# POOL's early arithmetic moved to DVE, and the rotary tables queued behind the rows' factors, in a hybrid decoder layer

## The chip, the core and the metric

The kernel runs on one core of a Trainium2 chip. Its engines work beside one another, each through its own queue in order: PE (matrix products; PEld is its loading of weights), DVE and ACT (work on whole tiles), POOL (the same, and DMAs of its own), SP (issues DMAs). The metric is the device time of one execution in microseconds; the profile is of one more execution, recorded instruction by instruction.

## What is computed

One decoder layer in float32 on 512 tokens of width 1024. The stretch that matters here is its beginning:

```python
u = rms_norm(h, norm_mix_g[l])
proj = u @ w_in[l]
conv_in, c_q, c_kv, k_rope_raw, gate_logits = jnp.split(proj, cut, axis=-1)
# conformer_conv, over conv_in: 512 channels, 31 taps
a, gt = jnp.split(conv_in, 2, axis=-1)
z = a * jax.nn.sigmoid(gt)
z = lax.conv_general_dilated(z, rhs, ..., feature_group_count=CONV_CH)
# rope_tables, used by the MLA attention
ang = positions.astype(jnp.float32)[..., None] * inv_freq
return jnp.cos(ang), jnp.sin(ang)
```

After it come the layer norm of the conv branch, the MLA attention, the gated merge, a cross-attention over 256 memory tokens and an MLP, with a final norm.

## The kernel before

**Products.** Every float32 product is made of three: each operand is split into a high half (rounded, on ACT, or scaled on ACT for x) and a low half (the rest, by a subtraction), and `mm3` (L231) sums high by high, low by high and high by low in one PSUM bank. `split` (L201) makes the two halves of weights: L202 is the copy on ACT, L203 the subtraction, on the engine `eng` or on DVE. `split_scaled` (L205) does the same for x times a norm's gain: L206 on ACT, L207 on DVE. PSUM has eight banks; products with the tag `mm` share four of them.

**First tile.** The loop at L610 goes over the eight 128-row slices k of x as they arrive: it splits the slice (`split_x`, L207 for the low half `ul`), splits the weights of the slices (`split` at L619, for k = 1, 2, 4, 6, with POOL for the low half), and PE multiplies at L622 into two banks, `fa` (the conv value) and `fg` (its gate). These are the first of the four channel tiles (index 0 to 3, `("ag", c)`).

**Rows' factors of x.** PE multiplies x without its RMS factor; the factor comes later. `x_stats` (L575) squares the slices on ACT (L577) and adds them up in turns on DVE and POOL (L579), and POOL adds the two sums into `nacc` (L580). `x_rows` (L582) sums `nacc` over the partitions on PE (L277), and DVE makes 1/sqrt from it in twelve small operations on 128x4 (L279, L245 to L250) into `rx`; a thirteenth makes `rx2` (L584). `x_bcast` (L586) spreads `rx` over the partitions with four transposes on PE (L271) and a copy on ACT to `rbx` (L588), evacuates the gate of tile 0 (`evac_g`, L599: L601 on DVE, the sigmoid L602 on ACT, L603 and L604 on DVE), and calls `rope_tables`.

**Rotary tables.** `rope_tables` (L439) makes the angles of the rotary embedding, reduced to one turn: 23 DVE operations on 128x4 to 128x64 (L440 to L462). `rope_sin` takes sine and cosine of them on ACT (L467, L468); nothing else reads them before the keys are turned, far later.

**Order.** PE's order is as written. `Pipe` (L337) prepares a unit's weights one unit ahead; `w_eng` is the engine of their subtraction: DVE for tile 1, POOL for tiles 2 and 3 and the units behind them. `after(ticks, fn)` (L214) puts work behind so many groups of three products: `x_bcast` stands five behind the row sums (D_X), hence in the middle of the gate of tile 1. The order on DVE, ACT and POOL is a planner's: it goes by readiness, by modelled durations and by the order in which the code writes the operations, and may put a later operation ahead of one that is not ready. The conv taps (`conv_taps`, L486: L492 once, L494 thirty times per tile, on DVE) run as background beside the products, and so do the gates' evacuations (L721) and the factors of the two latents (`latent_rows`, L669).

Of the kernel before, what the change touches and what calls it, by code (L numbers as in the profile page):

```python
# [19 lines left out]
ALU = mybir.AluOpType  # L20
# [148 lines left out]
def _body(tc, a):  # L169
# [3 lines left out]
    dve = nc.vector  # L173
    act = nc.scalar
    gps = nc.gpsimd
# [25 lines left out]
    def split(hi, lo, src, eng=None):  # L201
        act.copy(hi, src)  # L202
        (eng or dve).tensor_tensor(lo, src, hi.bitcast(F32), op=ALU.subtract)  # L203
# [14 lines left out]
    def tick(w):  # L218
        nonlocal bg
        clock[0] += w  # L220
        while later and later[0][0] <= clock[0] and not clock[2]:
            heapq.heappop(later)[2]()
        bg(w)
# [37 lines left out]
    rx = cst.tile([P, NT], F32, name="rx")  # L261
    rx2 = cst.tile([P, NT], F32, name="rx2")
# [5 lines left out]
    def bcast_rows(r, n=NT):  # L268
        b = bank("at")
        for t in range(n):  # L270
            pe.transpose(b[:, t * P:(t + 1) * P], r[:, t:t + 1].to_broadcast([P, P]), ident)  # L271
        return b

    def rstd_rows(sq, dim, dst=None):
        b = bank("at")
        for t in range(NT):
            pe.matmul(b[:, t:t + 1], sq[:, t * P:(t + 1) * P], ones1, start=True, stop=True)  # L277
        v = sm.tile([P, NT], F32, tag="rv", name="rv")
        dve.tensor_scalar(v, b[:, :NT], 1.0 / dim, EPS, op0=ALU.mult, op1=ALU.add)  # L279
        r = sm.tile([P, NT], F32, tag="rr", name="rr") if dst is None else dst  # L280
        rsqrt(r, v, NT)
        return r
# [11 lines left out]
    raws = {}  # L294
# [37 lines left out]
    w_eng = [dve]  # L332
# [32 lines left out]
    xr = xp.tile([P, KD, S], F32, name="xr")  # L365
    nacc = xp.tile([P, S], F32, name="nacc")
# [62 lines left out]
    def split_x(k):  # L429
        split_scaled(uh[:, k, :], ul[:, k, :], xr[:, k, :], v_("norm_mix_g", k))  # L430
# [8 lines left out]
    def rope_tables():  # L439
        dve.tensor_copy(posf, posi)  # L440
        fr = kon[:, K_FREQ:K_FREQ + n]
        for t in range(NT):
            sl = slice(16 * t, 16 * t + 16)
            dve.tensor_scalar(ang[:, sl], fr[:, sl], posf[:, t:t + 1], None, op0=ALU.mult)

        def fma(k, c):
            dve.scalar_tensor_tensor(ang, k, -c, ang, op0=ALU.mult, op1=ALU.add)

        dve.tensor_scalar(k_, ang, 1.0 / TWO_PI, MAGIC, op0=ALU.mult, op1=ALU.add)
        dve.tensor_scalar(k_, k_, MAGIC, None, op0=ALU.subtract)  # L450
        dve.tensor_scalar(kh, k_, 2.0 ** -11, MAGIC, op0=ALU.mult, op1=ALU.add)
        dve.tensor_scalar(kh, kh, MAGIC, 2048.0, op0=ALU.subtract, op1=ALU.mult)
        dve.tensor_tensor(k_, k_, kh, op=ALU.subtract)
        for c in PI_PARTS:
            fma(kh, c)
            fma(k_, c)
        dve.tensor_scalar(k_, ang, 1.0 / TWO_PI, MAGIC, op0=ALU.mult, op1=ALU.add)
        dve.tensor_scalar(k_, k_, MAGIC, None, op0=ALU.subtract)
        for c in PI_PARTS:
            fma(k_, c)  # L460
        dve.tensor_scalar(ang, ang, 3.1415925, -3.1415925, op0=ALU.min, op1=ALU.max)
        dve.scalar_tensor_tensor(k_, ang, -1.0, ang, op0=ALU.mult, op1=ALU.max)  # L462
# [103 lines left out]
    def proj_unit(key, c0, evac):  # L566
        def main(hl):
            b = bank()
            mm3(b, [(lhs(hl, k), (uh[:, k, :], ul[:, k, :])) for k in range(KD)])
            evac(b)  # L570
        pipe.unit(lambda: prep(key, c0=c0), main)

    hold = {}

    def x_stats():  # L575
        for k in range(KD):
            act.activation(xr[:, k, :], xr[:, k, :], AF.Square)  # L577
            if k > 1:
                (dve, gps)[k % 2].tensor_tensor(xr[:, k % 2, :], xr[:, k % 2, :], xr[:, k, :], op=ALU.add)  # L579
        gps.tensor_tensor(nacc, xr[:, 0, :], xr[:, 1, :], op=ALU.add)  # L580

    def x_rows():  # L582
        rstd_rows(nacc, D, rx)
        dve.tensor_tensor(rx2, rx, rx, op=ALU.mult)  # L584

    def x_bcast():  # L586
        b = bcast_rows(rx)
        act.copy(rbx, b)  # L588
        hold["a"] = fa
        evac_g(fg, 0)  # L590
        act.copy(identb, ident)
        act.copy(maskb, kon[:, K_MASK:K_MASK + 128])
        rope_tables()


    def evac_a(b, c):
        hold["a"] = b

    def evac_g(b, c):  # L599
        sg = wkp.tile([P, S], F32, tag="sg", name="sg")  # L600
        dve.tensor_tensor(sg, b, rbx, op=ALU.mult)  # L601
        act.activation(sg, sg, AF.Sigmoid)  # L602
        dve.tensor_tensor(sg, sg, rbx, op=ALU.mult)  # L603
        dve.tensor_tensor(zpad[:, c, CW - 1:], hold["a"], sg, op=ALU.mult)  # L604
        zready[0] = c + 1
# [4 lines left out]
    for k in range(KD):  # L610
        hl = first[k // 4]
        if k == 0:
            dve.tensor_copy(hl[0][:, 0], raws[0][:, 0])
            dve.tensor_tensor(hl[1][:, 0], raws[0][:, 0], hl[0][:, 0].bitcast(F32), op=ALU.subtract)
        split_x(k)
        if k == 1 or k > 0 and k % 2 == 0:
            kn = 1 if k == 1 else 2
            sl = slice(k % 4, k % 4 + kn)
            split(hl[0][:, sl], hl[1][:, sl], raws[0][:, k:k + kn], gps)  # L619
        for i, j in ((0, 0), (1, 0), (0, 1)):  # L620
            for b, c0 in ((fa, 0), (fg, 128)):
                pe.matmul(b, hl[i][:, k % 4, c0:c0 + 128], (uh, ul)[j][:, k, :],  # L622
                          start=k == 0 and i == j == 0, stop=k == KD - 1 and j == 1)
        tick(2.0)
    pipe.ahead(lambda: prep(("ag", 1), c0=0))
    x_stats()

    def evac_a1(b):
        x_rows()
        hold["a1"] = b  # L630
        after(D_X, x_bcast)
# [3 lines left out]
        evac_g(b, 1)  # L635

    for c in range(1, CT):
        w_eng[0] = dve if c == 1 else gps
        proj_unit(("ag", c), 0, evac_a1 if c == 1 else lambda b, c=c: evac_a(b, c))
        proj_unit(("ag", c), 128, evac_g1 if c == 1 else lambda b, c=c: evac_g(b, c))  # L640
    pipe.flush()
# [193 lines left out]
    for t in range(NT):  # L835
        b = bank()
        sl = slice(t * P, (t + 1) * P)
# [700 lines left out]
```

## Time and profile before

| | us |
|---|---|
| median of three runs | 796.04 (795.7 to 796.46) |
| the profiled execution | 797.19 |
| its span, first to last instruction | 795.4 |
| PE busy | 761.3 (96%) |
| DVE busy | 535.3 (67%) |
| ACT busy | 400.6 (50%) |
| POOL busy | 169.7 (21%) |

Busy time says how much of the span an engine worked, not whether anything waited for it. The chain of waits does: it is followed back from the last instruction to whatever released it. "Granted clock" is the share of TensorE's full 2.4 GHz that the chip gave PE in a stretch. The span begins with the loads of x and of the first weights, and the stretch that the change touches is its first 40 us.

### The profile page before, as it was taken

The page shows a single profiled execution, that of the slowest core. Times are in us where ns is not written, and L with a number is a line of the kernel's source. Part 1 is how long each engine was busy: PE and PEld are TensorE (multiplying, and loading weights), DVE is VectorE, ACT ScalarE, POOL GpSimd, SP SyncE. Part 2 cuts the span into 40 slices and gives each one's busy share as a digit, 9 for nine tenths or more (in the row PEclk, how much of TensorE's full clock was granted, in tenths as well). Part 3 has the DMA queues.
Part 4 walks back from the last instruction along what each step waited for, and adds up shares of the span by engine and source line. Part 5 has one row for each costly group of instructions (what it writes and reads, how often), then busy time and mean ns, then how long its engine had stood idle before and what let it go on. Part 6 is the DMA issues. An engine that isn't in the chain of part 4 may idle for free.

```text
span 795.4 us, 9520 instructions
## 1 busy us (share of the span) xinstructions
PE 761.3 (96%) x3594; PEld 627.8 (79%) x3594; DVE 535.3 (67%) x812; ACT 400.6 (50%) x681; POOL 169.7 (21%) x103
## 2 busy tenths in 40 slices
PE   8799999999999998998999999999999979999996
PEld 4589788778788886788887888888888858888785
DVE  5798999843888859758686833243333446667995
ACT  7323333469666537343465644444343445655562
POOL 4444336423312215346320000000000000111000
PEclk9899999999999999899999999999999998999998
DMA  8213223222102144124132324425353596999731
GB/s 280 97 40 113 76 84 128 84 90 97 54 0 107 54 157 162 58 102 146 68 105 106 118 108 146 171 82 224 106 188 129 165 283 239 227 236 213 198 106 53
DMA packets 26989, 103.36 MB, mean 130 GB/s; under 512 B 2368, under 2 KB 9920, under 8 KB 17984
## 3 DMA queue, kind: packets, MB, share of 16 engines
q1 hardware_dynamic: 13600, 67.54, 23.8%
q0 software_dynamic: 2304, 16.78, 10.4%
q10 hardware_dynamic: 11040, 18.45, 6.7%
q8 instruction: 28, 0.46, 0.2%
q14 instruction: 17, 0.14, 0.1%
HBM read 94.37 MB, written 8.39 MB: 129 GB/s over the span
## 4 chain that ended last, share of the span: by engine, by line
PE 70%; DVE 19%; DMA 4%; ACT 4%; issue 3%; SPq 0%; DVEq 0%; ACTq 0%
PE mm L239 18%; PE mm L237 18%; PE mm L238 18%; DVE cv L494 6%; PE at L238 4%; PE at L239 4%; PE at L237 4%; DMA a<-weights 2%; DVE q L203 1%; DVE mt L917 1%; DMA x<-weights 1%; DVE rs_t L248 1%; DMA xr<-xT 1%; PE at L810 1%; DVE sg L721 1%
## 5 line engine op out<-in xcount | busy, mean ns | idle before, releaser
L203 POOL TENSOR_TENSOR wl<-raw,wh 128x1024 fp32r<-128x1024 f32 (+4 forms) x65 | 144.6, 2227 | 252.4 <-ACT wh L202 249.3
L202 ACT CAST wh<-raw 128x1024 fp32r<-128x1024 f32 (+4 forms) x103 | 102.6, 998 | 190.0 <-PE mm L238 146.6
L203 DVE TENSOR_TENSOR wl<-raw,wh 128x1024 fp32r<-128x1024 f32 x38 | 46.5, 1224 | 99.6 <-ACT wh L202 99.6
L237 PE MATMUL mm<-hgh,wh 128*128 128x512 f32 x288 | 113.2, 393 | 0.0
L238 PE MATMUL mm<-hgl,wh 128*128 128x512 f32 x288 | 112.2, 390 | 0.0
L239 PE MATMUL mm<-hgh,wl 128*128 128x512 f32 x288 | 112.2, 390 | 0.0
L494 DVE SCALAR_TENSOR_TENSOR cv<-zpad,vec,cv 128x512 f32<-128x512 f32 x116 | 80.2, 752 | 0.1
L1356 POOL DMA_DIRECT2D x<-weights x12 | 10.6, 880 | 293.8 <-DVE wl L203 273.8
L237 PE MATMUL mm<-uh,wh 128*128 128x512 f32 x176 | 70.7, 402 | 2.3 <-DVE sg L721 2.1
L239 PE MATMUL mm<-uh,wl 128*128 128x512 f32 x176 | 69.3, 394 | 0.5 <-DVE wl L203 0.5
L238 PE MATMUL mm<-ul,wh 128*128 128x512 f32 x176 | 69.3, 394 | 0.0
L239 PEld LDWEIGHTS mm<-hgh,wl 128*128 128x128 f32 x288 | 54.1, 188 | 11.4
L237 PEld LDWEIGHTS mm<-hgh,wh 128*128 128x128 f32 x288 | 54.1, 188 | 10.9
L238 PEld LDWEIGHTS mm<-hgl,wh 128*128 128x128 f32 x288 | 54.1, 188 | 10.9
L203 DVE TENSOR_TENSOR wl<-x,wh 128x1024 fp32r<-128x1024 f32 x25 | 30.4, 1223 | 18.9 <-ACT wh L202 18.9
L237 PEld LDWEIGHTS mm<-uh,wh 128*128 128x128 f32 x176 | 33.5, 190 | 10.7 <-issue 4.2
L239 PEld LDWEIGHTS mm<-uh,wl 128*128 128x128 f32 x176 | 33.5, 190 | 8.1 <-DVE wl L203 1.0
L238 PEld LDWEIGHTS mm<-ul,wh 128*128 128x128 f32 x176 | 33.5, 190 | 6.5
L202 ACT CAST wh<-x 128x1024 fp32r<-128x1024 f32 x25 | 26.1, 1048 | 24.4 <-PE at L239 9.7
L238 PE MATMUL at<-wl,hA 128*128 128x512 f32 x96 | 37.6, 392 | 0.6 <-DVE wl L203 0.6
L239 PE MATMUL at<-wh,hB 128*128 128x512 f32 x96 | 37.4, 390 | 0.0
L237 PE MATMUL at<-wh,hA 128*128 128x512 f32 x96 | 37.4, 389 | 0.0
(392 smaller groups left out, 1772.4 us busy)
## 6 DMA issues: line engine op xcount, KB each, us to landing
raw<-weights SPq DMA_DIRECT2D x42, 1024.0 KB, 4.8
x<-weights POOLq DMA_DIRECT2D x12, 1024.0 KB, 11.4
a<-weights SPq DMA_DIRECT2D x5, 1024.0 KB, 8.3
x<-weights SPq DMA_DIRECT2D x4, 1024.0 KB, 5.9
raw<-weights SPq DMA_DIRECT2D x4, 768.0 KB, 4.3
xr<-xT SPq DMA_DIRECT2D x8, 256.0 KB, 6.0
raw<-weights SPq DMA_DIRECT2D x4, 512.0 KB, 5.0
ht<-xT ACTq DMA_DIRECT2D x1, 2048.0 KB, 9.4
```

Of the source, the lines that this page charges most:

```text
L202: act.copy(hi, src)
L203: (eng or dve).tensor_tensor(lo, src, hi.bitcast(F32), op=ALU.subtract)
L237: pe.matmul(out, wh, ah, start=first and i == 0, stop=False, **kw)
L238: pe.matmul(out, wh, al, start=False, stop=False, **kw)
L239: pe.matmul(out, wl, ah, start=False, stop=last and i == n - 1, **kw)
L248: dve.scalar_tensor_tensor(t, dst, -0.5, dst, op0=ALU.mult, op1=ALU.mult)
L494: dve.scalar_tensor_tensor(run if w < CW - 1 else acc[:, c, :], zs, wcol, run, op0=ALU.mult, op1=ALU.add)
L721: dve.tensor_tensor(t, b, rbx, op=ALU.mult)
L810: pe.transpose(b[:, (t - k) * P:(t - k + 1) * P], ptok[h, t][:, k * P:(k + 1) * P], ident)
L917: dve.tensor_tensor(t, t, gates[:, m, :], op=ALU.add)
L1356: gps.dma_start(out=t, in_=hbm(what, c), accum_op=ALU.add, max_dma_last_dim=8192)
```

## The change

Three things. All of POOL's arithmetic up to the weights of channel tile 2 goes to DVE: the additions of squares and their sum, the low halves of tile 0's weights, and those of tile 2 (POOL keeps tile 3 and what follows). The operations of `rope_tables` get an ordering edge behind the one that makes `rx2`: on DVE they can't be queued ahead of it. What is computed is the same.

```diff
+    rx_done = []
+
     def x_stats():
         for k in range(KD):
             act.activation(xr[:, k, :], xr[:, k, :], AF.Square)
             if k > 1:
-                (dve, gps)[k % 2].tensor_tensor(xr[:, k % 2, :], xr[:, k % 2, :], xr[:, k, :], op=ALU.add)
-        gps.tensor_tensor(nacc, xr[:, 0, :], xr[:, 1, :], op=ALU.add)
+                dve.tensor_tensor(xr[:, k % 2, :], xr[:, k % 2, :], xr[:, k, :], op=ALU.add)
+        dve.tensor_tensor(nacc, xr[:, 0, :], xr[:, 1, :], op=ALU.add)
 
     def x_rows():
         rstd_rows(nacc, D, rx)
-        dve.tensor_tensor(rx2, rx, rx, op=ALU.mult)
+        rx_done.append(dve.tensor_tensor(rx2, rx, rx, op=ALU.mult).ins)
...
-        rope_tables()
+
+        with tc.issue_after(rx_done[0]):
+            rope_tables()
...
-            split(hl[0][:, sl], hl[1][:, sl], raws[0][:, k:k + kn], gps)
+            split(hl[0][:, sl], hl[1][:, sl], raws[0][:, k:k + kn])
...
     for c in range(1, CT):
-        w_eng[0] = dve if c == 1 else gps
+        w_eng[0] = dve if c < 3 else gps
```

## Rows read from the trace of the kernel before

**Rows 1.** The page's chain that ended last: shares of the span by engine

```profile
PE 70%; DVE 19%; DMA 4%; ACT 4%; issue 3%; SPq 0%; DVEq 0%; ACTq 0%
```

**Rows 2.** Stretches in us: busy of each engine (instructions), granted clock, DMA share, GB/s

```profile
36.00:38.00 2.00, 2.00 (x7) 1.62 (x6) 0.69 (x1) 1.45 (x2) 0.00 (x0) 0.50 0.00 0
75.00:150.00 75.00, 72.58 (x367) 61.67 (x366) 75.00 (x123) 28.65 (x55) 34.70 (x24) 1.00 0.25 87
```

**Rows 3.** The chain in order of time: start, us, engine, tile, line

```profile
26.18 0.79 PE at L277 x8
...
30.53 4.88 issue
...
36.50 0.43 PE mm L237
...
39.49 0.37 PE mm L238
...
212.35 1.09 PE at L810 x10
```

**Rows 4.** Timeline of DVE: start, us, line, operation, out<-in, shape, count [idle before]

```profile
18.99 0.68 DVE L579 TENSOR_TENSOR xr<-xr 128x512 f32<-128x512 f32 x1
...
24.84 4.87 DVE L444 TENSOR_SCALAR ang<-kon,posf 128x16 f32<-128x16 f32 x4
...
32.70 0.15 DVE L279 TENSOR_SCALAR rv<-at 128x4 f32<-128x4 f32 x1
...
34.16 0.16 DVE L248 SCALAR_TENSOR_TENSOR rs_t<-rx 128x4 f32<-128x4 f32 x1
...
35.34 0.16 DVE L584 TENSOR_TENSOR rx<-rx 128x4 f32<-128x4 f32 x1
```

**Rows 5.** Single lines and tiles: shortest/median/longest in ns, first and last start in us

```profile
L207 DVE SCALAR_TENSOR_TENSOR ul<-xr,vec,uh x8: 739/784/1780, 4.6 to 17.3; 128x512 fp32r<-128x512 f32 x8
...
L444 DVE TENSOR_SCALAR ang<-kon,posf x4: 222/1262/2376, 24.8 to 29.5; 128x16 f32<-128x16 f32 x4
```

**Rows 6.** Timeline of POOL, 24 to 30 us

```profile
24.74 4.80 POOL L203 TENSOR_TENSOR wl<-raw,wh 128x1024 fp32r<-128x1024 f32 x2
```

**Rows 7.** Groups on DVE up to 40 us: count, busy us, mean ns, idle before

```profile
L207 DVE SCALAR_TENSOR_TENSOR ul<-xr,vec,uh 128x512 fp32r<-128x512 f32 x8 | 8.9, 1142 | 3.8 <-ACT uh L206 3.8
...
L579 DVE TENSOR_TENSOR xr<-xr 128x512 f32<-128x512 f32 x3 | 3.9, 1288 | 0.3 <-ACT xr L577 0.3
...
L203 DVE TENSOR_TENSOR wl<-raw,wh 128x1024 fp32r<-128x1024 f32 x2 | 2.4, 1212 | 0.0
```

**Rows 8.** Timeline of PE: the slice k = 2, and the unit behind tile 0

```profile
9.73 0.73 PE L622 MATMUL mm<-uh,wh 128*128 128x512 f32 x2 [1.09 <-ACT uh L206]
...
20.86 0.50 PE L239 MATMUL mm<-uh,wl 128*128 128x512 f32 x1 [0.54 <-DVE wl L203]
```

**Rows 9.** Timeline of ACT, 25 to 40 us

```profile
25.99 1.05 ACT L202 CAST wh<-raw 128x1024 fp32r<-128x1024 f32 x1 [3.98 <-PE mm L238]
...
33.83 0.26 ACT L467 ACTIVATE cs<-ang 128x64 f32<-128x64 f32 x1 [5.49 <-DVE ang L461]
...
36.53 0.59 ACT L588 COPY rbx<-at 128x512 f32<-128x512 f32 x1 [2.10 <-PE at L271]
37.14 1.28 ACT L602 ACT_TABLE_LOAD   x1
38.43 0.63 ACT L602 ACTIVATE sg<-sg 128x512 f32<-128x512 f32 x1
```

**Rows 10.** Timeline of DVE from 37 us: the operations with a wait before them

```profile
37.16 0.69 DVE L601 TENSOR_TENSOR sg<-mm,rbx 128x512 f32<-128x512 f32 x1 [1.65 <-ACT rbx L588]
40.12 0.69 DVE L601 TENSOR_TENSOR sg<-mm,rbx 128x512 f32<-128x512 f32 x1 [2.28 <-PE mm L239]
...
67.53 1.89 DVE L603 TENSOR_TENSOR sg<-sg,rbx 128x512 f32<-128x512 f32 x1 [2.51 <-ACT sg L602]
```

**Rows 11.** A group on DVE, 68 to 150 us

```profile
L248 DVE SCALAR_TENSOR_TENSOR rs_t<-rr 128x4 f32<-128x4 f32 x6 | 6.4, 1074 | 0.0
```

## The prediction

> **What bounds the kernel now.** The page's chain comes first: PE carries 70% of what ended last, DVE 19% [rows 1]. So time is won only where PE stands still or runs slowly, or where DVE decides when PE may go on. Two stretches show where that is [rows 2]: between 75 and 150 us PE is busy for 72.6 of 75 us, and DVE is full as well; between 36 and 38 PE is full, but the granted clock is 0.50, which is 1.2 GHz.
>
> The chain in order of time says why [rows 3]. L277, the row sums of nacc, ends at 26.97; fifteen matmuls more end at 30.53; then come 4.88 us of nothing, until the transposes of L271, which spread rx over the partitions, start at 35.41. After this standstill PE runs at half clock: eight matmuls take 0.43 us each in place of 0.23, the last one a little less, and full speed is back at 39.85.
>
> PE is waiting for DVE. L277 is done at 26.97, but L279, the first of the thirteen small operations that turn its sums into rx and rx2, starts at 32.70, and L584, the last, ends at 35.50 [rows 4]. Ahead of it and between them in DVE's queue stand the rotary tables (L440 to L462, 23 operations). They are tiny: an operation of 128x16 at L444 takes 0.22 us at its shortest. Yet another took 2.38 [rows 5], and the four 4.87 us together [rows 4]. Beside them POOL ran two subtractions of 128x1024, from 24.74 to 29.54 [rows 6]. The same shows earlier: L207 (128x512) takes 0.74 us at its shortest and 1.78 at its longest [rows 5], where POOL was busy with its own part of the first tile.
>
> **Part one: POOL's arithmetic goes to DVE.** Moved are four subtractions for the first channel tile (L619: one of 128x256, three of 128x512), three additions of squares (L579) and their sum (L580), and both subtractions of the tile with index 2 (128x1024). DVE takes 0.68 us for 512 columns at 18.99 [rows 4] and 1.21 for 1024 [rows 7]; for 256 I estimate 0.4 from these two. That adds 0.4 + 7 x 0.68 + 2 x 1.21 = 7.6 us. What DVE gets back, if POOL's neighbourhood is the cause: eight L207 at 1.14 on average against a median of 0.78, 8 x 0.36 = 2.9; three L579 at 1.29 against 0.68, 1.8 [rows 5, 7]; four L444 at 4.87 together against 4 x 0.22, 4.0. That is 8.7, so DVE is 1.1 us lighter in all. No DMA moves with the operations. SP's loads of weights wait for the last reader of their buffer, which is now a shorter operation.
>
> In the first tile PE needs six matmuls per k, 1.38 us at 0.23. It took up k = 2 at 9.73 [rows 8]; six groups without a hole end at 18.0, and two matmuls of the next unit at 18.5. Before, the third matmul of that unit, which needs the low half of its weights, began at 20.86 after a wait of 0.54 [rows 8]. So at most 2.4 us can come here. Whether they do depends on DVE between 9.7 and 18 us: six L207 (4.6), two low halves (1.4) and that of the next unit (1.2) make 7.2 of 8.3, with additions of squares put into the gaps by a planner I can't see. I take 1.8, between 0.3 (the additions get in the way) and 2.4.
>
> **Part two: the tables stand behind rx2.** Nothing is removed; 23 operations go behind the thirteen of the rows. The thirteen cost 0.2 us each, since the last seven ran from 34.16 to 35.50 [rows 4]; rx is there after twelve, 2.4 us. From the end of L277 PE has fifteen matmuls, 3.56 us, before it wants rx [rows 3]. So rx comes about a microsecond early, and the whole 4.88 us goes. One 128x1024 subtraction of the tile with index 2 may sit among the thirteen: its ACT half starts at 25.99, when PE lets go of the buffer, close to L277 [rows 9]. Then rx is 0.2 late. Also nacc must be there when L277 comes. What has to stand ahead of it on DVE after 9.7 us is the 7.2 above and seven additions of 0.68, 12.0; with the other half of the next unit, 1.2, it ends near 23, and L277 would come at 18.5 + 22 x 0.23 = 23.6. I take 4.8, between 3.5 and 4.9.
>
> The clock: without the standstill PE has no reason to fall to 1.2 GHz. The four transposes took 1.09 us, from 35.41 to 36.50; ten at L810 take 1.09 at full clock, so 0.65 comes back. Eight matmuls from 36.50 to 39.86 took 3.36 in place of 1.84, another 1.5 [rows 3]. Together 2.1, between 0 (the clock falls for another reason) and 2.2.
>
> **What hides the tables now.** Behind rx2 they cost DVE 23 operations, about 5.2 us at 0.22, in a stretch where DVE waited 1.65 us for rbx and 2.28 for PE [rows 10]. Behind them stand the evacuations L601 to L604 and the taps. Later DVE waited 2.51 us more, for the gate of the tile with index 3 [rows 10]. These three waits are the cover: 6.4 us, against 5.2 of tables and 1.2 of subtraction. With PE about 8 us earlier, the first two of them shrink by what stage one wins and no more, so I count DVE at most 1.4 us late at the third. Of that 1.2 is free: L603 took 1.89 us there beside a POOL subtraction, 1.2 above its 0.68, and would be held to that one's end anyway [rows 10]. From there DVE is full to 150 us, so what it is late is paid. Six L248 there take 1.07 us on average [rows 11] against 0.15, because each chain of row factors meets POOL operations. Shifted against POOL, a chain may meet one more or one less, 1.9 us either way. I give back 0.4, between -2 and 3. If the cover were gone altogether the tables and the subtraction would cost 6.4. Past 150 PE is the chain again and everything shifts together.
>
> **Sum.** 1.8 + 4.8 + 2.1 - 0.4 = 8.3 us, against the profiled execution of 797.19 (span 795.4 and 1.8 around it). That one lies 1.15 above the median of the runs, 796.04, so I predict 796.0 - 8.3 = 787.7. A difference of 0.2%, 1.6 us, is about what a measurement of this kernel can tell from no change.
>
> **The rivals.** *Another queue's head.* Only the tables' place behind rx2 is fixed; PE's order is written out, while DVE's and ACT's come from the planner. The first matmul of the tile with index 2 needs a bank, and all four are taken; L601 frees one. After the transposes come ACT's copy (0.59) and L601 (0.69), with their handovers 1.35 us [rows 9, 10]; PE has nine matmuls, 2.06. If all tables stand ahead of L601, it is done 2.7 us too late, and with up to 2.1 for the clock the gain is 3.5 to 5.6, some 791.5. If ACT's Sin (L467), which needs the tables, stands ahead of the copy to rbx, as it does now [rows 9], 3.9 us are lost, and the time is near 793. For it: that is today's order. Against it: Sin's input came before rx, and now comes five microseconds later. Sin between two sigmoids costs ACT two table loads of 1.28 and 0.6 of its own, 3.2 us; a cast of 1.05 and POOL's 2.4 leave 2 us of the 5.5 of a unit, so about one may show. The Trainium skill's page "ScalarE: Activation LUTs", section "What ACT_TABLE_LOAD costs", counts 2.66 us for a switch, of which 1.28 is the load; by that ACT would lose 5.9 and three to four would show, 791. Here the sigmoid starts right behind its load [rows 9], so I don't use it.
>
> *Given back in the taps.* DVE falls behind, and the stretch to 150 us takes most of it: gain 0 to 2, time 795. DVE is full there, which speaks for it; the lighter sum and the cover speak against.
>
> *Slower: DVE can't carry it.* If the long operations were not POOL's doing, DVE gets 7.6 us of work and nothing back. It then reaches its full stretch later by 7.6 less its waits, all of them (6.4) or all but that for PE (4.1): 1.2 to 3.5 us, time near 798.5. It decides once less than 1.2 of the 8.7 comes back. For it: DVE is full to 150 us as it is [rows 2]. Against it: 0.22 and 2.38 in one row, for the same shape [rows 5]. The Trainium skill's page "SBUF — State Buffer", section "Who interferes with whom", says that POOL and a DVE operation with two SBUF inputs or in a two-port mode shut each other out for a whole instruction; the 2.38 us of a 16-column operation beside POOL's 2.40 agree, and for that I hold this chance low.
>
> *It doesn't do what it says.* Something else keeps rx late, and nothing changes: 796.
>
> **Chances.** Forecast (gain 6.5 to 10.5) 0.70; another queue's head 0.16; given back 0.05, of which 0.03 is within 0.2%; no change 0.03; slower 0.06. The range 785.0 to 792.5 takes in the bounds of the terms that pull the same way and most of the queue rival. Faster 0.88, same 0.06, slower 0.06.
>
> **What will show it.** POOL without arithmetic until the casts of the tile with index 3; every L207 near 0.75; L279 right behind L277; no standstill of PE ahead of L271, and a granted clock of 1.00 from 20 to 40 us. L440 behind L584, its operations at 0.2. Then DVE without its waits up to the gate of index 3, and about 8 us less at each later stage. I am wrong if PE waits for a bank at the tile with index 2, if L277 waits for nacc, or if PE's idle time between 75 and 150, 2.4 us now, grows by what was won.

## The result, and the profile after the change

| | before | after |
|---|---|---|
| median of the runs, us | 796.25 | 788.77 (787.82 to 790.5) |
| ratio, 95% interval | | 0.9899 (0.9876 to 0.9922) |
| the profiled execution, us | 797.19 | 788.28 |
| its span, us | 795.4 | 786.5 |
| DVE busy, us | 535.3 | 532.9 |
| POOL busy, us | 169.7 | 152.7 |

The forecast was 787.7, within 785.0 to 792.5. The kernel is faster by 7.5 us between the medians and by 8.9 between the two profiled executions.

Stretches of the changed kernel: start:end and length, then PE, PEld, DVE, ACT and POOL busy (instructions), granted clock, DMA share, GB/s.

```profile
20.00:40.00 20.00, 20.00 (x95) 16.46 (x95) 17.32 (x48) 6.45 (x10) 2.58 (x2) 1.00 0.27 94
75.00:150.00 75.00, 72.01 (x365) 60.90 (x364) 73.25 (x121) 28.82 (x50) 33.45 (x24) 1.00 0.25 86
```

PE is busy for every microsecond between 20 and 40, at full clock: the standstill of [rows 3] and the half clock of [rows 2] are both gone. Between 75 and 150 PE works 72.0 us against 72.6 [rows 2], so a little of what was won is lost there.

The chain in order of time, changed kernel (start, us, what):

```profile
24.55 0.79 PE at L277 x8
...
27.55 0.23 PE mm L237
...
28.91 0.54 PE at L271 x4
29.45 0.23 PE mm L237
```

Against [rows 3] the row sums L277 start 1.63 us earlier, the transposes L271 6.50 earlier, and these take 0.54 in place of 1.09.

The same place on DVE (timeline: start, us, line, operation, out<-in, shape, count, [idle before]):

```profile
21.46 0.68 DVE L582 TENSOR_TENSOR nacc<-xr 128x512 f32<-128x512 f32 x1
...
25.38 0.16 DVE L279 TENSOR_SCALAR rv<-at 128x4 f32<-128x4 f32 x1 [2.10 <-PE at L277]
...
26.26 1.22 DVE L203 TENSOR_TENSOR wl<-raw,wh 128x1024 fp32r<-128x1024 f32 x1
...
28.56 0.16 DVE L250 SCALAR_TENSOR_TENSOR rx<-rs_t,rx 128x4 f32<-128x4 f32 x1
28.76 0.16 DVE L586 TENSOR_TENSOR rx<-rx 128x4 f32<-128x4 f32 x1
28.84 0.16 DVE L440 CAST posf<-posi 128x4 f32<-128x4 int32 x1
29.04 0.64 DVE L444 TENSOR_SCALAR ang<-kon,posf 128x16 f32<-128x16 f32 x4
...
30.28 0.68 DVE L605 TENSOR_TENSOR sg<-mm,rbx 128x512 f32<-128x512 f32 x1
...
33.01 2.13 DVE L447 SCALAR_TENSOR_TENSOR ang<-k__164,ang 128x64 f32<-128x64 f32 x1
```

(Lines from 575 on are shifted by 2 to 4; L586 is the L584 of before, L605 its L601.) L279 now waits for PE and starts 0.04 us after the sums. The thirteen operations follow at 0.20 each, with one 128x1024 subtraction among them; rx is there at 28.72, just before L271. The four L444 take 0.64 together; they took 4.87 [rows 4]. L440 comes behind L586. L605, the evacuation of the first gate, isn't queued behind all the tables: it runs after the eighth of them.

POOL up to 35 us, and the first tile's low halves of x on DVE (shortest/median/longest in ns, first and last start in us):

```profile
1.40 0.10 POOL L427 MEMSET cs<- 128x4 f32 x1
32.66 2.40 POOL L203 TENSOR_TENSOR wl<-raw,wh 128x1024 fp32r<-128x1024 f32 x1 [31.15 <-ACT wh L202]
```

```profile
L207 DVE SCALAR_TENSOR_TENSOR ul<-xr,vec,uh x8: 741/746/753, 4.8 to 16.1; 128x512 fp32r<-128x512 f32 x8
```

POOL has nothing to compute for 31 us, and none of the eight L207 is over 0.75 us; in [rows 5] the longest took 1.78. At 33.01 a table operation of 64 columns takes 2.13 us: it stands beside POOL's first subtraction.

PE's waits between 60 and 170 us (engine, tile, line <- what ended them: us in total, times, longest):

```profile
PE mm L237 <- DVE sg L725: 2.1, 2, 1.2
PE mm L237 <- DVE rs_t L248: 0.9, 1, 0.9
```

L725 is the evacuation of a gate. The matmul that is said to wait for L248 doesn't read L248's row factor; it needs a bank, and an L725 ends just ahead of L248, at 81.60 us, so this wait too is likely one for a gate's evacuation.

### The profile page after: what moved, and what is told of

Read it like the earlier page. It is cut to its first block, busy times and chain, and to the rows that moved or that the text cites. A ratio compares the mean times of both kernels' runs of the same rounds, so it can differ in the third digit from the quotient of the medians.

```text
span 786.5 us, 9521 instructions
## 1 busy us (share of the span) xinstructions
PE 758.8 (96%) x3594; PEld 627.1 (80%) x3594; DVE 532.9 (68%) x822; ACT 400.4 (51%) x681; POOL 152.7 (19%) x93
## 4 chain that ended last, share of the span: by engine, by line
PE 71%; DVE 18%; DMA 4%; ACT 4%; issue 2%; SPq 0%; ACTq 0%; DVEq 0%
PE mm L237 18%; PE mm L239 18%; PE mm L238 18%; DVE cv L494 6%; PE at L238 4%; PE at L239 4%; PE at L237 4%; DMA a<-weights 2%; DVE q L203 1%; DVE mt L921 1%; DMA x<-weights 1%; DMA xr<-xT 1%; PE at L814 1%; DVE rr L250 1%; DVE rs_t L248 1%
## 5 line engine op out<-in xcount | busy, mean ns | idle before, releaser
L203 POOL TENSOR_TENSOR wl<-raw,wh 128x1024 fp32r<-128x1024 f32 (+2 forms) x59 | 135.2, 2293 | 263.1 <-ACT wh L202 255.2
L203 DVE TENSOR_TENSOR wl<-raw,wh 128x1024 fp32r<-128x1024 f32 (+2 forms) x44 | 51.4, 1169 | 100.1 <-ACT wh L202 100.1
L494 DVE SCALAR_TENSOR_TENSOR cv<-zpad,vec,cv 128x512 f32<-128x512 f32 x116 | 80.3, 742 | 0.1
```

The costliest lines, as they stand in the source:

```text
L494: dve.scalar_tensor_tensor(run if w < CW - 1 else acc[:, c, :], zs, wcol, run, op0=ALU.mult, op1=ALU.add)
```

## The experiments

### Either part alone

The forecast gave 1.8 us to the first part (POOL's arithmetic), 4.8 to the second (the order of the tables), and 2.1 to the clock. Four kernels take the change apart. The first has the ordering edge alone:

```diff
+            rx_done.append(dve.tensor_tensor(rx2, rx, rx, op=ALU.mult).ins)
...
+        with tc.issue_after(rx_done[0]):
+            rope_tables()
```

> Only the ordering edge: the rotary tables stand behind rx2, POOL keeps all its arithmetic. Theory A (rx was late for two causes, either of which makes it late by itself: the tables ahead of the rows in DVE's queue, and POOL's subtractions holding up DVE's operations beside them): L279 starts right behind L277, near 27.0 us, but two of the thirteen row operations meet POOL's two subtractions (24.7 to 29.5), so rx comes near 31 and PE stands still for 0.3 to 1.2 us in place of 4.9; no fall of the clock; the first tile as before. 5.5 to 6.5 us less than before. Theory B (the order in the queue alone was the cause): no standstill, 7 us less. Theory C (POOL alone was the cause): PE still stands still for 3 us or more, at most 2 us less.

The second has POOL's arithmetic moved and no edge:

```diff
-        gps.tensor_tensor(nacc, xr[:, 0, :], xr[:, 1, :], op=ALU.add)
+        dve.tensor_tensor(nacc, xr[:, 0, :], xr[:, 1, :], op=ALU.add)
...
-            split(hl[0][:, sl], hl[1][:, sl], raws[0][:, k:k + kn], gps)
+            split(hl[0][:, sl], hl[1][:, sl], raws[0][:, k:k + kn])
...
-        w_eng[0] = dve if c == 1 else gps
+        w_eng[0] = dve if c < 3 else gps
```

> Only the move of POOL's arithmetic to DVE, no ordering edge: the planner puts four of the tables' lines ahead of L279 and the rest between the row operations. Theory A: the tables run at 0.2 us each, L279 starts within 0.3 us of L277's end, the interleaved rows take 3 to 4.5 us with one 128x1024 subtraction among them, rx comes near 29.5 and PE stands still for 0.5 to 1.5 us; the first tile is 1.6 us shorter, the clock doesn't fall; 7 to 8 us less than before, so the edge itself is worth about one. Theory B (order alone): 2 us less, with the standstill of nearly 5 us and the half clock still there. Theory C (POOL alone): the same 8.3 as the whole change.

The third moves the weights of the tile with index 2 alone (the last hunk of these), the fourth the first tile's and the squares' operations alone (all but the last hunk).

> Only the two subtractions of the channel tile with index 2 go to DVE; POOL keeps the first tile and the sums of squares, and there is no edge. Theory A: these two were what the tables ran beside; the four operations of L444 now take under 1 us together in place of 4.87, rx comes near 31.5, PE stands still for 0.7 to 2 us, no or little half clock; 4 to 6 us less than before, with the first tile unchanged. If the four stay at 4.9 us, POOL isn't what holds them up.

> Only the first tile's low halves and the sums of squares go to DVE; the subtractions of the tile with index 2 stay on POOL and there is no edge. Theory A: every L207 near 0.75 us and L277 1.6 us earlier; the tables start earlier too, near 22 us, but meet one POOL subtraction, and the rows meet the other, so rx comes between 30 and 31 where PE wants it at 28.8: a standstill of 1 to 2.5 us, and 3.5 to 6 us less in all. If DVE could not carry the additions, L277 would be no earlier than 26.0.

Measured, the four beside the same runs of the kernel before (median 797.25), the changed kernel beside runs of its own (796.25). Times in the columns are starts in the trace, in us; the last matmul column is the first product of the query latent:

| | L277 starts | standstill before L271 | then at clock 0.50 | query latent | median, ratio to before |
|---|---|---|---|---|---|
| before | 26.02 | 4.88 | 6.8 us | 61.68 | 797.25 |
| edge alone | 26.29 | 1.08 | none | 57.16 | 792.67, 0.9939 (0.9919 to 0.9959) |
| tile 2's weights alone | 26.64 | 2.00 | 3.4 us | 59.03 | 793.92, 0.9950 (0.9933 to 0.9967) |
| first tile and squares alone | 24.85 | 2.59 | 3.4 us | 57.86 | 793.15, 0.9932 (0.9908 to 0.9957) |
| all of POOL's, no edge | 24.87 | 0.29 | none | 53.95 | 788.45, 0.9886 (0.9859 to 0.9913) |
| the change | 24.39 | none | none | 53.10 | 788.77, 0.9899 (0.9876 to 0.9922) |

With POOL quiet and no edge nearly all of the change is there. In DVE's queue tables and rows' factors take turns, with the 128x1024 subtraction among them, and still the last row operation is only a little late:

```profile
25.86 0.16 DVE L279 TENSOR_SCALAR rv<-at 128x4 f32<-128x4 f32 x1 [0.86 <-PE at L277]
25.93 0.18 DVE L451 TENSOR_SCALAR kh<-k__164 128x64 f32<-128x64 f32 x1
26.05 0.17 DVE L245 TENSOR_SCALAR rs_i<-rv 128x4 int32<-128x4 int32 x1
...
29.64 0.15 DVE L584 TENSOR_TENSOR rx<-rx 128x4 f32<-128x4 f32 x1
```

L584 ended at 35.50 before [rows 4]. So the tables were in the way because POOL stretched them, more than because of where they stood: with POOL quiet, 18 of the 23 still stand ahead of and between the thirteen, and PE loses 0.3 us.

The edge alone shows the other half. DVE and POOL with POOL's subtractions still there:

```profile
27.47 2.34 DVE L245 TENSOR_SCALAR rs_i<-rv 128x4 int32<-128x4 int32 x1
```

```profile
25.04 4.75 POOL L203 TENSOR_TENSOR wl<-raw,wh 128x1024 fp32r<-128x1024 f32 x2
```

The tables are out of the way, and now a row factor of four columns is held to the end of POOL's second subtraction: 2.34 us for what takes 0.17. PE stands still for 1.08 us. The hold falls on what DVE has in its queue at that moment: tables before, a row factor here.

This kernel has a second loss. L604, which evacuates the first gate and with it frees a bank for the tile with index 2, comes behind thirteen of the tables, at 34.49, and PE waits for it:

```profile
35.23 0.50 PE L237 MATMUL mm<-uh,wh 128*128 128x512 f32 x1 [0.66 <-DVE sg L604]
```

The two halves of POOL's move each leave a piece of it. Tile 2's weights alone (DVE, then POOL):

```profile
23.08 3.44 DVE L203 TENSOR_TENSOR wl<-raw,wh 128x1024 fp32r<-128x1024 f32 x2
...
29.30 0.15 DVE L279 TENSOR_SCALAR rv<-at 128x4 f32<-128x4 f32 x1
```

```profile
23.30 2.15 POOL L580 TENSOR_TENSOR nacc<-xr 128x512 f32<-128x512 f32 x1 [0.69 <-DVE xr L579]
```

Two subtractions that need 2.4 us take 3.44 beside POOL's sum, and the tables behind them hold L279 until 29.30. These tables run at 0.2 each, as expected, yet L277 is done at 27.59: where they stand does count once DVE comes to them late. The first tile alone (DVE):

```profile
22.51 2.37 DVE L440 CAST posf<-posi 128x4 f32<-128x4 int32 x1
...
26.06 2.33 DVE L451 TENSOR_SCALAR kh<-k__164 128x64 f32<-128x64 f32 x1
...
28.94 0.15 DVE L279 TENSOR_SCALAR rv<-at 128x4 f32<-128x4 f32 x1
```

Two table operations of 0.2 lose 2.1 to 2.2 us each to POOL's two subtractions. So the parts are not a sum: counted at the first product of the query latent, the edge alone brings 4.52 us, the POOL part alone 7.73, both 8.58. Either alone takes most of one and the same standstill.

Between the medians the edge alone brought 4.6 us (5.5 to 6.5 expected), tile 2's weights 3.3 (4 to 6, with little or no half clock), the first tile and the squares 4.1 (3.5 to 6), and all of POOL's 8.8, more than the 7 to 8 that were expected with a standstill of 0.5 to 1.5. Three of the four sizes were missed.

The edge was timed once more: the changed kernel and the one without the edge, side by side.

> The changed kernel itself, timed beside the next run on the same chip to settle what the ordering of the tables is worth once POOL is quiet. Theory (nothing): within 0.8 us of the next run. Rival (the edge brings 1 us or more, as the forecast had it): shorter than the next run by 1 us or more.

> The kernel before with POOL's work of the first three tiles moved to DVE and no ordering of the tables. Theory: within 0.8 us of the changed kernel beside it, near 788.6 us. Rival: longer than it by 1 us or more.

Measured: 789.33 (784.26 to 790.32), ratio 0.9895 (0.9870 to 0.9920), and 787.28 (786.71 to 787.93), ratio 0.9878 (0.9862 to 0.9893). The intervals overlap; the medians lie 2.05 us apart, more than the 0.8 expected, and the kernel with the edge is the slower one. In the traces PE reaches the transposes of the key latent 8.32 us earlier than before with the edge and 8.53 without; in the first pair it was 8.24 and 8.13. (The start of L277 alone differs by 0.6 us between four profiles with the same first tile, 26.02 to 26.64, and every such lead carries that.) Counted from L277, the way to those transposes takes 123.3 us in both profiles with the edge, and 122.9 and 123.0 without. So the edge brings nothing that these runs can show. It saves PE the 0.3 us before L271 and gives back 0.7 between 75 and 150 us: there the wait put down to L248 is 0.9 us with the edge, in both profiles, and 0.2 without it, in both.

### Is it POOL, and what of POOL?

Up to here POOL's part in it was read from coincidence: long operations stand beside POOL's. The next kernel puts POOL to work in the changed kernel, with data that nobody else uses.

```diff
     gps.memset(cs[:, :, 32:33], 1.0)
+    dm = wp.tile([P, 2, S], F32, name="dm")
+    gps.memset(dm, 0.0)
+    for _ in range(20):
+        gps.tensor_tensor(dm[:, 1, :], dm[:, 0, :], dm[:, 1, :], op=ALU.add)
```

> The changed kernel with twenty additions of 128x512 on POOL from about 2 us on, on a tile of their own that nobody else reads: no data and no order tie them to the rest, and they only read two inputs from SBUF each, some 26 us in all by the 1.27 us that such an addition took on POOL in the kernel before. Theory (what made DVE late in the kernel before was POOL reading beside it, not the work that POOL held): DVE's 128x512 differences of line 207 go back from 0.70-0.75 us to 0.8-1.8 us, the last matmul of the first tile's unit goes from 24.4 to 25 us or more, PE stands still before the transposes of line 271 again by over 1 us, and the time is 791 to 796 us. Rival (DVE was late because it waited for POOL's results): differences stay at 0.70-0.75 us, no standstill, and the time is within 1 us of the changed kernel's 788.8.

Measured: 806.31 us (805.82 to 808.03), ratio 1.0109 (1.0083 to 1.0134). That is 17.5 us over the changed kernel and slower than the kernel before. POOL's rows, then DVE's L207, then PE's waits up to 45 us, then a stretch:

```profile
2.48 32.10 POOL L431 TENSOR_TENSOR dm<-dm 128x512 f32<-128x512 f32 x20
```

```profile
L207 DVE SCALAR_TENSOR_TENSOR ul<-xr,vec,uh x8: 1745/1764/1835, 5.2 to 28.3; 128x512 fp32r<-128x512 f32 x8
```

```profile
PE mm L630 <- DVE ul L207: 5.1, 3, 2.6
PE mm L239 <- DVE wl L203: 3.2, 1, 3.2
PE mm L630 <- DVE wl L622: 2.4, 1, 2.4
```

```profile
36.00:41.00 5.00, 5.00 (x12) 3.85 (x12) 3.73 (x5) 0.00 (x0) 0.00 (x0) 0.50 0.43 120
```

Every L207 takes 1.76 us in place of 0.75. DVE and POOL take turns, instruction by instruction: from one start of DVE to the next pass 1.69 us (9.73 to 11.42, say), and POOL's additions take 1.6 each where 1.27 was expected. The direction was as the theory had it, the place and the size (791 to 796 us) were not: with the additions beside the whole first tile PE waits there already and in the unit behind it, 10.7 us in these rows, and what it works between its waits is partly at half clock, as from 36 to 41. L277 comes at 43.70 in place of 24.39.

The same with fills, which write but read nothing:

```diff
+    for _ in range(20):
+        gps.memset(dm, 0.0)
```

> The changed kernel with twenty fills of 128x1024 on POOL from about 2 us on, on a tile of their own: POOL is as busy as with the twenty additions or nearly so, but it reads nothing. Theory (it is the reading of two inputs that holds up DVE): DVE's differences of line 207 stay at 0.70-0.80 us and the time stays within 1 us of the changed kernel's 788.8. Rival (anything that POOL does beside DVE holds it up): differences of 1.0 us or more, a standstill before line 271, and 791 us or more.

```profile
2.45 20.22 POOL L431 MEMSET dm<- 128x1024 f32 x20
```

```profile
L207 DVE SCALAR_TENSOR_TENSOR ul<-xr,vec,uh x8: 731/746/752, 5.5 to 16.4; 128x512 fp32r<-128x512 f32 x8
```

Measured: 789.35 us (788.0 to 790.62), ratio 0.9892 (0.9865 to 0.9920). For 20 us POOL is as busy as can be beside the first tile, and no L207 loses anything. So for an operation with two inputs in SBUF, as L207 is, it is not a busy POOL that holds DVE up, but a POOL that reads. The Trainium skill's page "SBUF — State Buffer", section "Who interferes with whom", says so: a DVE instruction with two SBUF inputs contends with a GpSimd instruction that reads SBUF, "not with one that only writes it". These two runs agree, 1.76 and 0.75 us. The page also counts in copies, casts and operations with a scalar in their two-port modes; the row factor of four columns that took 2.34 and the cast that took 2.37 are of these kinds.

For a cast the fills alone are enough. One stands beside them, that of the first weights (128x256). In the run with the fills (DVE, POOL), then in the changed kernel:

```profile
4.66 0.91 DVE L621 CAST wh<-raw 128x256 fp32r<-128x256 f32 x1 [4.66 <-DMA raw<-weights]
```

```profile
4.47 0.95 POOL L431 MEMSET dm<- 128x1024 f32 x1
```

```profile
4.28 0.29 DVE L617 CAST wh<-raw 128x256 fp32r<-128x256 f32 x1 [4.28 <-DMA raw<-weights]
```

It starts within a fill, ends just behind it, at 5.57, and takes three times as long as alone; PE waits 0.8 us for it. What fills do to the tables and the row factors no run here shows, since the fills end at 22.7 and they come later.

### What DVE's load costs, and what is left

The forecast gave back 0.4 us for DVE's load up to 150 us. One kernel leaves the tables out:

```diff
     def rope_tables():
-        dve.tensor_copy(posf, posi)
...
+        dve.tensor_copy(ang, kon[:, K_FREQ:K_FREQ + n])
+        dve.tensor_copy(k_, kon[:, K_FREQ:K_FREQ + n])
```

> The changed kernel with the rotary tables' arithmetic left out (their two results are copies of the frequencies, two small DVE instructions in place of 27 or so), so that DVE has some 5 us less to do between 28 and 44 us. Theory (the tables are hidden behind the taps, and DVE's load there costs PE nothing soon): within 0.6 us of the changed kernel. Rival (DVE is full from 25 us to 150 us, so every microsecond of load comes back as PE idle time between 75 and 150 us): PE idle time there falls from 3.0 us to under 1 us and the time falls by 1.5 to 3 us.

Measured: 787.57 (783.86 to 789.23), ratio 0.9868 (0.9825 to 0.9911); the interval takes in the changed kernel's. The trace is sharper. PE's waits from 36 to 150 us:

```profile
PE mm L237 <- DVE sg L704: 2.1, 2, 1.2
PE mm L237 <- DVE rs_t L248: 0.2, 1, 0.2
```

The wait for L248 falls from 0.9 to 0.2, and from L277 to the transposes of the key latent PE gains 0.67 us on the changed kernel (0.29 behind it at the one, 0.38 ahead at the other). So leaving the tables out of the changed kernel brings about 0.7 us, which lies between the two theories. That it is DVE's load which costs the 0.7 isn't shown: the kernel without the edge has the tables too and waits 0.2 us at that place, and so does the next kernel, in which DVE has 2.4 us more to do. The waits of 2.1 for the gates don't come from the tables.

The next moves the fourth tile's weights to DVE too, so that POOL stays quiet to 45 us:

```diff
-        w_eng[0] = dve if c < 3 else gps
+        w_eng[0] = dve
...
+    w_eng[0] = gps
     pipe.flush()
```

> The changed kernel with the fourth tile's two 128x1024 weight differences on DVE as well (1.22 us each there, 2.40 us each on POOL), so that POOL stays quiet to 45 us. DVE gets 2.4 us of work, and the two instructions of line 447 that were held up beside POOL (2.13 and 2.00 us, against 0.2 alone) give back 3.7 us. Theory (what DVE carries and what POOL holds up nearly cancel, and PE waits for neither there): within 0.8 us of the changed kernel, line 447 without an instruction over 0.4 us. Rival (DVE is at its limit, and its added work comes out in PE's idle time between 75 and 150 us, 3.0 us in the changed kernel): slower by 1 to 2.5 us.

Measured: 788.38 (786.4 to 790.16), ratio 0.9880 (0.9851 to 0.9908), the same as the changed kernel; no L447 is over 0.23 us. But PE now waits for DVE at the tile:

```profile
PE mm L239 <- DVE wl L203: 0.6, 1, 0.6
```

It waits less for L248 later (0.2 us), and is 0.57 us behind the changed kernel at the transposes of the key latent. So between 25 and 75 us the change stops where DVE still has room: with two subtractions more, PE begins to wait.

The last look is at the stretch to 150 us. In the changed kernel five small operations there take about 2 us, each beside one of POOL's subtractions for the gates' weights. These five go to DVE:

```diff
     for i in range(16):
...
+        w_eng[0] = dve if i in (3, 4, 8, 9, 10) else gps
         proj_unit(("gate", i // 2), 128 * (i % 2), lambda b, i=i: evac_gate(b, i))
```

> The changed kernel with five of the gates' 128x1024 weight differences taken from POOL to DVE as well: gates 3, 4, 8, 9 and 10, the ones beside which five of DVE's row-factor instructions between 75 and 135 us took 2 us instead of 0.15. It adds 5 times 1.22 = 6.1 us to DVE and gives back 5 times some 1.9 = 9.5. Theory (what is left of PE's 3.0 us of idle time between 75 and 150 us comes from those held-up instructions): idle time there falls to 1 to 2 us, and the time falls by 0.5 to 2 us. Rival (DVE's queue, full with the taps, is what makes those waits): the added 6.1 us make the idle time 3 us or more, and the time is the same or up to 2 us longer.

Measured: 785.06 us (780.99 to 786.46), ratio 0.9842 (0.9820 to 0.9864), beside the changed kernel's 789.33 and 0.9895 (0.9870 to 0.9920) on the same chip. It is faster than the kernel before and than the changed kernel, by 4.3 us against the latter, where 0.5 to 2 was expected. Its stretch, and the operation that starts near 76.5 us in the changed kernel and in this one:

```profile
75.00:150.00 75.00, 75.00 (x384) 64.26 (x383) 70.83 (x128) 30.23 (x52) 23.82 (x19) 1.00 0.26 92
```

```profile
76.58 2.23 DVE L246 TENSOR_SCALAR rr<-rs_i 128x4 int32<-128x4 int32 x1
```

```profile
76.48 0.17 DVE L246 TENSOR_SCALAR rr<-rs_i 128x4 int32<-128x4 int32 x1
```

PE has no idle time left between 75 and 150 us, and DVE, with five subtractions of 1.2 us more, is busy for 70.8 us in place of 73.3: it gets back more than it is given. At the transposes of the key latent PE is 3.87 us ahead of the changed kernel; 3.0 of that are the idle time, and for the rest the records name no wait.

Does that cost arise only with the change? The same edit on the kernel before:

> The kernel before with the five gates' weight differences (3, 4, 8, 9, 10) on DVE and nothing else of the change: does POOL's hold on DVE cost by itself at 75 to 150 us, or only once the change has filled DVE? Theory (it costs by itself): PE's idle time between 75 and 160 us, some 2.4 us, goes to 0.5 us or less, the early standstill stays at 4.9 us, and the time is 793 to 794 us, 2 to 3 us below the kernel before. Rival (the change made that idle time): within 1 us of the kernel before.

```profile
75.00:150.00 75.00, 75.00 (x383) 64.87 (x382) 73.87 (x131) 30.68 (x57) 24.40 (x20) 1.00 0.26 92
```

Measured: 794.58 (792.95 to 795.6), ratio 0.9951 (0.9934 to 0.9969), 3.4 us below its own runs of the kernel before (2 to 3 expected), with a standstill of 5.0 us before L271 as ever. The 2.4 us of idle time go here as well. So the kernel before paid them too; the change made them only a little larger.

## Why the prediction was right, and where it wasn't

**The total** was 1.1 us too low against the median, and the profiled execution gained 8.9 where the sum said 8.3. At the transposes of the key latent the lead is 8.24 us, and 8.43 at 618 us; the rest comes in the MLP behind that, which the change doesn't touch: one wait of PE there, 5.59 us before and 4.63 after, lies anywhere from 4.1 to 5.7 in the profiles of this case. That part is luck.

**Part one** was forecast at 1.8 us; L277 starts 1.63 earlier. The eight L207 give back what was counted: they have a median of 0.746 without an exception, against 1.14 on average [rows 7]. PE's wait for the weights of the unit behind tile 0 fell from 0.54 [rows 8] to 0.3; nacc was ready at 22.14, before it was needed. DVE's busy time fell by 2.4 us in all, where 1.1 was forecast.

**Part two** is the step that failed. It said that the whole 4.88 us go because the tables stand behind rx2. They go, but with POOL quiet and no edge 4.59 of them go too. The rows could have said so: four L444 at 4.87 beside POOL's 4.80 [rows 4, 6] lose 4.0 us to it (L440, at 23.55 just ahead of them, takes 1.25 in place of 0.16 beside POOL's sum). Take these 4.0 from 35.50, where L584 ended, and it ends at 31.5 with the tables still ahead of it, a microsecond after PE's 30.53; so the order was worth about 1 us once POOL was quiet, and 0.29 was measured. The forecast did count the 4.0, but as load taken from DVE in part one, and didn't ask what they did to the standstill. The sum is not touched by this, since the standstill stands in it once; what to do with the kernel next is. That the edge alone also brings 3.8 of the 4.88 makes the two parts rivals for one gain.

**The clock** was forecast at 2.1. From L271 to the first product of the query latent PE gains 2.0 more (a lead of 6.59 us, then 8.58). It goes with the standstill and not with a part: the kernel without the edge gains the same 2.0 behind L271 (5.74, then 7.73), the two half moves, which leave a standstill of 2.0 and 2.6, 0.4 each (2.25, then 2.65; 3.46, then 3.82). The edge alone gains only 1.0 (3.52, then 4.52), though at full clock: there the first product of the tile with index 2 waits for L604 and starts 1.05 us behind the matmul ahead of it, in place of 0.23.

**The cover.** Forecast: DVE's waits of 6.4 us [rows 10] are used up by 5.2 of tables (23 at 0.22 are 5.1) and 1.2 of subtraction, and 0.4 is given back. DVE has not one wait from L279 to 75 us, and the lead falls from 8.58 to 8.24: 0.34. Without the tables 0.7 comes back.

**Rivals.** The bank for the tile with index 2 didn't come late: L605 runs after eight tables, not after all. That this rival is real the edge alone shows: there the evacuation came behind thirteen, and PE waited 0.66 us for the bank. ACT's Sin did come between two sigmoids, as feared; the first runs at 43.15 behind a table load at 39.76, the next sigmoid needs another, and PE doesn't wait:

```profile
39.76 1.28 ACT L467 ACT_TABLE_LOAD   x1
43.15 0.26 ACT L467 ACTIVATE cs<-ang 128x64 f32<-128x64 f32 x1 [2.11 <-DVE ang L461]
...
45.09 1.28 ACT L606 ACT_TABLE_LOAD   x1
```

"DVE can't carry it" was held low on the ground that POOL's reading makes the operations long; the twenty additions show that this ground holds.

**The stretch to 150 us** was taken as DVE's own limit, paid by whatever DVE is late, although the forecast saw that POOL lengthens L248 there. The gates' run shows that this is wrong: DVE was full there because POOL held it, and PE's idle time in it, 2.4 us before and 3.0 after, goes when five subtractions change their engine.

## What to carry to other kernels

When an operation takes far longer than its like, look at what POOL does at that moment, and above all at what it reads, and take that away before reordering the queue: the order decides only which operation is held. Two causes of one standstill must not be added; ask of each what remains if the other alone is removed. An engine that is busy 98% of a stretch may be held and not loaded; its longest operations tell which, against the shortest of the same shape.

## What the runs showed of the hardware

A DVE operation of 128x4, 0.17 us alone, took 2.0 to 2.4 us beside a POOL subtraction of 128x1024 (2.40 alone), whether it had one SBUF input (L245, L246, the cast L440) or two (L248 at 83.71 us of the changed kernel, 1.99). The conv taps L494, with one input in SBUF and one in PSUM, have 0.74 us each beside the same subtractions. POOL loses as well: an addition of 128x512 took 1.6 us between DVE's, and 2.1 in the kernel with the edge alone. Fills of 128x1024 on POOL left L207 at 0.75 us, but a cast of 128x256 beside one took 0.91 in place of 0.29.

In the stretch that the change touches PE ran at half clock not at all after a standstill of 0.29 or 1.08 us, for 3.4 us after 2.00 and 2.59, and for 6.8 us after 4.88 and 5.0. The length of the standstill alone doesn't settle it, as later places of the same traces show: 2.28 us of waiting were followed by no half clock in the kernel before (at 377.94) and by 3.4 us of it with the edge alone (at 374.03); 3.07 went with 6.8 us of it in the kernel before (at 317.47), 3.05 with 3.4 in the kernel with the additions (at 328.54). In the kernel before 2.6 of the 6.8 us lay in the standstill itself, from 32.8 to 35.4. In these runs, therefore, a standstill of 2.0 cost nearly as much in clock as one of 4.88: shortening it to 2.0 to 2.6 brought 0.4 us behind L271, and removing it 2.0.
